# Opening stage of a two-layer trunk: modulation rows as four column-group products among the first part's, and the first part done one stream at a time

## The chip, the cores and the metric

The kernel runs on one core of one Trainium2 chip. The metric is the device time of one execution in microseconds (us), median of three runs. The engines are TensorE (PE in the rows, with its weight loads as PEld), VectorE (DVE), ScalarE (ACT), GpSimd (POOL) and SyncE (SP, which here only issues transfers).

## What is computed

Two layers run over 256 latent tokens ("x") and, in the first layer, 256 context tokens ("ctx"), each of width 1024. Every sub-layer is normalised and modulated by a shift and a scale that are products of a conditioning vector with `w_mod`. The opening stage computes the first modulation rows and the first tiles of the first feed-forward product:

```
silu_c = jax.nn.silu(c)
silu_cc = jax.nn.silu(c_ctx)
...
m = (silu_c @ w_mod[i] + b_mod[i]).reshape(b, 1, N_MOD, d)
mc = (silu_cc @ w_mod[i] + b_mod[i]).reshape(1, 1, N_MOD, d)
...
def modulate(x, g, shift, scale):
    return rms_norm(x, g) * (1 + scale) + shift

def swiglu(h, w13, w2):
    a, b = jnp.split(h @ w13, 2, axis=-1)
    return (jax.nn.silu(a) * b) @ w2
```

The rest (attention with pooling, a gated mixer, three more feed-forward blocks) is the same in both kernels.

## The kernel before

Activations lie transposed: 8 parts (k = 0 to 7) of 128 features, each with 512 columns, of which the first 256 are the latent stream and the last 256 the context stream. Large products are done in three matmuls: every fp32 operand is split into a rounded high part and a rest (`whi`/`wlo` or `sh`/`sl` for weights, `AH`/`AL` for activations; ACT rounds, DVE subtracts), and `mm3` adds wlo·AH, whi·AH and whi·AL in PSUM.

`start()` holds four weight tile pairs ("f" = 0 to 3, two tiles each, eight PSUM banks `pss`) and walks over the eight parts in the hand-written `order`. For part i of that order it needs its weights (512 KB, `raw4`, two buffers, split into hi and lo) and its normalised and modulated activations: DVE multiplies by `rb` (the reciprocal root mean square), ACT applies scale and shift into `h`, ACT rounds to `AH`, DVE subtracts to `AL`. Then 24 matmuls follow.

Scale and shift reach `mod` in two ways. For parts 0 to 4 DVE multiplies rows of `w_mod` (512 KB transfers, `wm`) with the conditioning vector, `cc`, and sums along the row (`use_mod`, L80): two rows by two streams for each part. For parts 5, 6 and 7 (`by_rows`) PE multiplies the 2-column conditioning vector by w_modr, four transfers of 768 KB with two of the eight contraction steps each (`wn`, lying in buffers called raw, raw, whi, wlo), 16 fp32 products of 384 columns (L697) that give 2 rows; ACT copies the rows out (L701), PE turns them into columns (L704), DVE copies them to `mod` (L707).

Ahead of that PE spreads the conditioning vector to `cc` (L665) and adds up the squares for the normalisation (L680). Order on an engine comes from a scheduler; where the code says `keep_in_program_order` (`pin`) it does not move. SP issues transfers in one queue, in program order, each behind the buffer that it overwrites. After `start()` the first feed-forward block goes on with tile pair f = 4 from `load_w`.

Of the kernel before, what the change touches and what calls it, by code (L numbers as in the profile page):

```python
# [16 lines left out]
P = 128  # L17
# [8 lines left out]
NR = 3  # L26
# [9 lines left out]
def trunk(ctx: ExitStack, tc: tile.TileContext, I, out):  # L36
# [8 lines left out]
    def bank():  # L45
        return pp.tile([P, 512], F32, name="ps")
# [592 lines left out]
    def start():  # L639
        ng = 4  # L640
        order = (0, 5, 1, 6, 2, 7, 3, 4)
        with tc.tile_pool(name="start", bufs=1) as sp:
# [6 lines left out]
            cT = sp.tile([P, 2, NK], F32, name="cT")  # L649
            nc.sync.dma_start(out=cT, in_=I["cT"])  # L650
# [5 lines left out]
            S.activation(out=cT, in_=cT, func=AF.Silu)  # L656

            S.activation(out=rb[:, 0:1], in_=cT[:, 0, 0:1], func=AF.Sqrt, scale=0.0, bias=epsb)

            for st in range(2):  # L660
                for h in range(2):
                    ps = bank()
                    for k4 in range(4):
                        k = 4 * h + k4
                        PE.matmul(ps[:, k4 * P:k4 * P + P], cT[:, st, k:k + 1].broadcast_to([P, P]),  # L665
                                  ident, start=True, stop=True)
# [14 lines left out]
            S.activation(out=rb, in_=ps, func=AF.Sqrt, scale=1.0 / D, bias=epsb)  # L681
# [3 lines left out]
            V.reciprocal(rb, rb)  # L685
# [5 lines left out]
            def by_rows():  # L691

                row = sp.tile([2, 2 * NR * P], F32, name="row")
                ps = [bank() for _ in range(2)]
                for k in range(NK):
# [4 lines left out]
                for j in range(2):  # L700
                    S.copy(row[:, j * NR * P:(j + 1) * NR * P], ps[j][0:2, :NR * P])  # L701
                ps = bank()
                for i in range(2 * NR):
                    PE.matmul(ps[:, 2 * i:2 * i + 2], row[:, i * P:i * P + P], ident[0:2, 0:2],  # L704
                              start=True, stop=True)
                for st in range(2):
                    V.tensor_copy(mod[:, st, :16].rearrange("p (j k) -> p j k", j=2)[:, :, NK - NR:],  # L707
                                  ps[:, 0:4 * NR].rearrange("p (j k s) -> p s j k", j=2, k=NR)[:, st])
                finish_mod(0, 0, 2, slice(NK - NR, NK))

            by_rows()
            pss = [[bank(), bank()] for _ in range(ng)]
            nxt = 1
            for i, k in enumerate(order):
                raw = raws.get(k) or get_raw(k)
                split(sh[:, k], sl[:, k], raw[:, :2])
                split(wh[0][:, k], wl[0][:, k], raw[:, 2])
                split(wh[1][:, k], wl[1][:, k], raw[:, 3])
                xr = tmp.tile([P, 2 * T], F32, name="sa", bufs=2)
                h = tmp.tile([P, 2 * T], F32, name="h32", bufs=2)  # L720
                V.tensor_tensor(out=xr, in0=X[:, k], in1=rb, op=ALU.mult)
                for st in range(2):
                    ts = slice(st * T, st * T + T)
                    S.activation(out=h[:, ts], in_=xr[:, ts], func=AF.Identity,
                                 scale=gs[:, st, 0, k:k + 1], bias=mod[:, st, k:k + 1])
# [6 lines left out]
                split(AH[:, k, :2 * T], AL[:, k, :2 * T], h)  # L732

                def products(f, k, first, last):
                    for ab in range(2):
                        cs = slice(ab * P, ab * P + P)
                        w = (sh[:, k, f, cs], sl[:, k, f, cs]) if f < 2 else \
                            (wh[f - 2][:, k, cs], wl[f - 2][:, k, cs])
                        mm3(pss[f][ab], *w, AH[:, k, :2 * T], AL[:, k, :2 * T], first, last)

                for f in range(ng):
                    products(f, k, i == 0, i == NK - 1)
# [17 lines left out]
def _pack(x, c, ctx, c_ctx, w_mod, b_mod, norm_g, ffn_w13, ffn_w2, w_in_a, qk_norm_g, pool_w,  # L760
# [5 lines left out]
    r["cT"] = ac(np.stack([c[0], c_ctx]).reshape(2, NK, P).transpose(2, 0, 1))  # L766
# [72 lines left out]
```

## Time and profile before

| what | value |
|---|---|
| median of 3 runs | 1141.48 us (1141.21 to 1141.87) |
| profiled execution | 1142.17 us |
| its span on the core | 1140.4 us |
| PE busy in the span | 1132.2 us (99%) |
| DVE, ACT, POOL busy | 863.6, 522.0, 68.4 us |
| granted TensorE clock | 1.00 |

The profiled execution took 1.8 us more than its span (what lies ahead of the first and behind the last instruction) and 0.7 us more than the median. The stage that changes is the first 73 us of the span. A matmul's duration in a row holds its way through the array; how fast matmuls follow each other is read from their starts.

### The profile page before, as it was taken

The numbers are of one execution on the slowest core, as the hardware profiler recorded it, in microseconds if no ns is written. First come the engines' busy times: TensorE is split into PE (matmuls) and PEld (weight loads), VectorE is DVE, ScalarE is ACT, GpSimd is POOL, SyncE is SP. The second block draws the span as 40 slices with busy tenths as digits, with TensorE's granted clock in tenths as the row PEclk, the third lists the DMA queues.
The fourth block names the chain that finished last, engine by engine and source line by source line (L and its number), as shares of the span: only waits on it lengthen the run. The fifth ranks groups of instructions, "written<-read, shape, count | busy, mean of one in ns | idle before, by whom it ended". The sixth has DMA issues, their size and how long they took to land.

```text
span 1140.4 us, 19165 instructions
## 1 busy us (share of the span) xinstructions
PE 1132.2 (99%) x7696; PEld 1033.9 (91%) x7696; DVE 863.6 (76%) x1582; ACT 522.0 (46%) x816; POOL 68.4 (6%) x140
## 2 busy tenths in 40 slices
PE   8999999999999999999999999999999999999998
PEld 4888888888888897899999999999999899999998
DVE  5967787878789979777778887656667788756663
ACT  5552212223223357664335456435445866434442
POOL 0000111122222200000000000000000000000000
PEclk9999999999999999999999999999999999999999
DMA  8844656788888850556687566456447536546543
GB/s 323 310 148 156 197 186 234 279 282 325 294 297 306 305 196 11 222 172 223 212 305 264 187 219 218 161 167 219 174 143 257 185 114 219 176 154 237 178 143 114
DMA packets 52408, 242.72 MB, mean 213 GB/s; under 512 B 5600, under 2 KB 11488, under 8 KB 38880
## 3 DMA queue, kind: packets, MB, share of 16 engines
q1 hardware_dynamic: 33888, 174.39, 43.4%
q0 software_dynamic: 18432, 67.12, 17.4%
q8 instruction: 60, 0.98, 0.4%
q14 instruction: 28, 0.23, 0.1%
HBM read 240.44 MB, written 1.05 MB: 212 GB/s over the span
## 4 chain that ended last, share of the span: by engine, by line
PE 97%; DVE 1%; ACT 1%; DMA 1%; issue 0%; SPq 0%; DVEq 0%; ACTq 0%
PE ps L148 30%; PE ps L149 30%; PE ps L150 30%; PE ps L697 1%; PE ps L618 1%; PE ps L619 1%; PE ps L617 1%; PE ps L680 1%; PE ps L665 1%; DMA raw<-in_w_out_a 0%; ACT whi L153 0%; PE ps L501 0%; PE ps L469 0%; DVE st L473 0%; PE ps L172 0%; ACT pe L477 0%
## 5 line engine op out<-in xcount | busy, mean ns | idle before, releaser
L148 PE MATMUL ps<-AH,wlo 128*128 128x258 f32 (+2 forms) x1664 | 507.1, 305 | 0.3 <-ACT AH L153 0.3
L149 PE MATMUL ps<-AH,whi 128*128 128x258 f32 (+2 forms) x1664 | 506.6, 305 | 0.0
L150 PE MATMUL ps<-AL,whi 128*128 128x258 f32 (+2 forms) x1664 | 505.5, 305 | 0.0
L153 ACT CAST whi<-raw 128x1024 fp32r<-128x1024 f32 (+2 forms) x354 | 313.7, 921 | 363.7 <-PE ps L150 260.3
L154 DVE TENSOR_TENSOR wlo<-raw,whi 128x1024 fp32r<-128x1024 f32 (+2 forms) x354 | 367.6, 1064 | 54.4 <-ACT whi L153 53.4
L148 PEld LDWEIGHTS ps<-AH,wlo 128*128 128x128 f32 x1664 | 316.3, 190 | 16.1 <-issue 1.1
L149 PEld LDWEIGHTS ps<-AH,whi 128*128 128x128 f32 x1664 | 314.3, 189 | 14.7 <-issue 0.5
L150 PEld LDWEIGHTS ps<-AL,whi 128*128 128x128 f32 x1664 | 313.4, 189 | 14.5 <-issue 0.2
L150 PE MATMUL ps<-HL,whi 128*128 128x256 f32 (+1 forms) x704 | 218.0, 310 | 0.0
L149 PE MATMUL ps<-HH,whi 128*128 128x256 f32 (+1 forms) x704 | 218.0, 310 | 0.0
L148 PE MATMUL ps<-HH,wlo 128*128 128x256 f32 (+1 forms) x704 | 218.0, 310 | 0.0
L80 DVE CUSTOM_DVE_ANT_0 wm<-wm,cc 128x1024 f32<-128x1024 f32 x138 | 164.7, 1219 | 6.1 <-DMA wm<-in_w_mod 5.0
L148 PEld LDWEIGHTS ps<-HH,wlo 128*128 128x128 f32 x704 | 132.5, 188 | 7.8
L150 PEld LDWEIGHTS ps<-HL,whi 128*128 128x128 f32 x704 | 132.5, 188 | 7.7
L149 PEld LDWEIGHTS ps<-HH,whi 128*128 128x128 f32 x704 | 132.6, 188 | 7.7
L72 POOL DMA_DIRECT2D wm<-in_w_mod x128 | 67.7, 529 | 546.2 <-DVE mod L80 508.6
L206 ACT ACTIVATE sa<-sa,cb 128x256 f32<-128x256 f32 x66 | 33.6, 510 | 119.7 <-DVE sa L205 116.4
L246 DVE SCALAR_TENSOR_TENSOR X<-ps,gate,X 128x256 f32<-128x256 f32 x64 | 30.9, 482 | 48.0 <-PE ps L150 47.9
L204 DVE COPY cb<-ps 128x1 f32<-128x1 f32 x66 | 10.3, 155 | 72.8 <-PE ps L150 72.7
L212 DVE TENSOR_TENSOR h<-ps,sa 128x512 f32<-128x512 f32 x22 | 15.2, 692 | 43.4 <-PE ps L150 34.2
L80 DVE CUSTOM_DVE_ANT_0 junk<-wm,cc 128x1024 bf16<-128x1024 f32 x34 | 41.4, 1218 | 8.6 <-ACT cc L667 7.2
L154 DVE TENSOR_TENSOR HL<-h,HH 128x256 fp32r<-128x256 f32 (+1 forms) x88 | 42.3, 485 | 0.0
(162 smaller groups left out, 705.3 us busy)
## 6 DMA issues: line engine op xcount, KB each, us to landing
raw<-in_w SPq DMA_DIRECT2D x84, 1024.0 KB, 4.9
wm<-in_w_mod POOLq DMA_DIRECT2D x128, 512.0 KB, 5.0
raw<-in_w SPq DMA_DIRECT2D x64, 704.0 KB, 4.1
wm<-in_w_mod SPq DMA_DIRECT2D x10, 512.0 KB, 6.4
raw<-in_w_in_a SPq DMA_DIRECT2D x5, 1024.0 KB, 7.8
raw<-in_w SPq DMA_DIRECT2D x8, 512.0 KB, 5.3
raw<-in_w_out_a SPq DMA_DIRECT2D x4, 1024.0 KB, 5.0
raw<-in_w_in_cu SPq DMA_DIRECT2D x4, 1024.0 KB, 4.8
```

What stands on the lines that cost most here:

```text
L72: eng.dma_start(out=w, in_=I["w_mod"][layer, i])
L80: pin(V.tensor_tensor_reduce(out=res, in0=w, in1=cc[:, st, :], scale=1.0, scalar=0.0, op0=ALU.mult, op1=ALU.add, accum_out=mod[:, 2 * laye ...
L148: PE.matmul(ps, wl, xh, start=first, stop=False)
L149: PE.matmul(ps, wh, xh, start=False, stop=False)
L150: PE.matmul(ps, wh, xl, start=False, stop=last)
L153: S.copy(hi, src)
L154: pin(V.tensor_tensor(out=lo, in0=src, in1=hi.bitcast(F32), op=ALU.subtract))
L206: S.activation(out=sa[:, :T], in_=sa[:, :T], func=AF.Silu, bias=cb[:, 0:1])
L212: V.tensor_tensor(out=h32[:, :n], in0=ps[1][:, :n], in1=sa[:, :n], op=ALU.mult)
L246: V.scalar_tensor_tensor(out=X[:, m, :T], in0=ps[:, :T], scalar=gate[:, 2 * layer, sub, m:m + 1], in1=X[:, m, :T], op0=ALU.mult, op1=ALU.add)
L617: PE.matmul(ps[b], AL[:, k, ts], hi[:, ws], start=(k == 0), stop=False)
L618: PE.matmul(ps[b], AH[:, k, ts], hi[:, ws], start=False, stop=False)
```

## The change

- The conditioning vector is kept as 32 columns for each contraction step (`c32`, two real ones and 30 zeros), so that a product fills 32 rows of its output. Step k goes to the rows 32·g to 32·g+31 of a bank, with g = k mod 4: four products stand side by side in a bank, in four groups of array columns. The `row` tile has 128 rows, and a small selector matrix (`sel`, loaded together with the conditioning vector as `cs`) adds the four groups up when the rows are turned (L715 of the changed kernel).
- Of the code's order, the products of the rows (L707) stand behind the first part's roundings and ahead of its matmuls; the first part (i = 0) is done a stream (256 columns) at a time, first three tile pairs, for one stream and then the other, then the fourth pair. All that leads to it is cut in halves as well: root, reciprocal, normalisation, and `AH` comes straight from ACT.
- The `raw4` of part 0 and that of the second part are issued ahead of w_modr and of the next `wm`. The order of parts is 0, 5, 6, 1, 7, 2, 3, 4 instead of 0, 5, 1, 6, 2, 7, 3, 4, and the 24 matmuls of a middle part go hi·AH, lo·AH, hi·AL over all tiles. The `use_mod` work stands behind the matmuls of its part.

```
-        order = (0, 5, 1, 6, 2, 7, 3, 4)
+        order = (0, 5, 6, 1, 7, 2, 3, 4)
...
+            c32 = sp.tile([P, NK, 32], F32, name="c32")
+            V.memset(c32, 0.0)
...
-            S.activation(out=cT, in_=cT, func=AF.Silu)
+            S.activation(out=c32[:, :, 0:2], in_=cs[:, :2 * NK].rearrange("p (k s) -> p k s", k=NK),
+                         func=AF.Silu)
...
+            raws = {0: get_raw(0)}
             for i in range(4):
                 nc.sync.dma_start(out=wn[i], in_=I["w_modr"][:, 2 * i:2 * i + 2])
-            raws = {0: get_raw(0)}
+            raws[order[1]] = get_raw(order[1])
             wm.update({(1, h): load_mod(0, 2 + h, nc.sync) for h in range(2)})
-            raws[order[1]] = get_raw(order[1])
...
-            S.activation(out=rb, in_=ps, func=AF.Sqrt, scale=1.0 / D, bias=epsb)
+            halves = [slice(st * T, st * T + T) for st in range(2)]
+            for ts in halves:
+                S.activation(out=rb[:, ts], in_=ps[:, ts], func=AF.Sqrt, scale=1.0 / D, bias=epsb)
...
+            def rows():
+                for r in range(2):
                     for j in range(2):
-                        PE.matmul(ps[j][0:2, :NR * P], cT[:, :, k],
-                                  wn[k // 2][:, k % 2, j * NR * P:(j + 1) * NR * P],
-                                  start=k == 0, stop=k == NK - 1)
...
+                        for g in range(4):
+                            k = 4 * r + g
+                            PE.matmul(psr[j][32 * g:32 * g + 32, :NR * P], c32[:, k],
+                                      wn[k // 2][:, k % 2, j * NR * P:(j + 1) * NR * P],
+                                      start=r == 0, stop=r == 1)
...
-                    PE.matmul(ps[:, 2 * i:2 * i + 2], row[:, i * P:i * P + P], ident[0:2, 0:2],
+                    PE.matmul(ps[:, 2 * i:2 * i + 2], row[:, i * P:i * P + P], sel,
...
+            for ts in halves:
+                pin(V.reciprocal(rb[:, ts], rb[:, ts]))
+                pin(V.tensor_tensor(out=xr0[:, ts], in0=X[:, order[0], ts], in1=rb[:, ts],
+                                    op=ALU.mult))
...
+                if i == 0:
+
+                    for ts in halves:
+                        normed(ts, AH[:, k, ts])
+                        normed(ts, h[:, ts])
+                        if ts.start == 0:
+                            for j in range(2):
+                                pin(S.copy(row[:, j * NR * P:(j + 1) * NR * P], psr[j][:, :NR * P]))
+                    for ts in halves:
+                        pin(V.tensor_tensor(out=AL[:, k, ts], in0=h[:, ts],
+                                            in1=AH[:, k, ts].bitcast(F32), op=ALU.subtract))
...
+                if i == 0:
+                    for fs, ts in ((range(ng - 1), 0), (range(ng - 1), 1), ((ng - 1,), 0), ((ng - 1,), 1)):
...
+                if 0 < i < NK - 1:
+                    for a, x in ((0, AH), (1, AH), (0, AL)):
+                        for f in range(ng):
+                            for ab in range(2):
+                                PE.matmul(pss[f][ab], tile_of(f, ab, k)[a], x[:, k, :2 * T],
+                                          start=False, stop=False)
```

Three places show what the scheduler makes of it. The rows name the operation, out<-in and the output's size, and in brackets the engines and transfers that it waits for (DMAHW0 is the transfer of the conditioning vector).

ACT at the very start, before:

```order
L656 ACT_TABLE_LOAD
L656 ACTIVATE cT<-cT 128x16 [waits DMAHW0_49]
L658 ACT_TABLE_LOAD [waits DVE_49]
L658 ACTIVATE rb<-cT,epsb 128x1 [waits Activation_49]
L667 COPY cc<-ps 128x512 [waits PE_49]
```

The same of the changed kernel (c_87 is `c32`):

```order
L660 ACT_TABLE_LOAD [waits DMAHW0_49]
L660 ACTIVATE c_87<-cs 128x8x2 [waits DVE_49]
L663 ACT_TABLE_LOAD
L663 ACTIVATE rb<-c_87,epsb 128x1 [waits Activation_49]
L672 COPY cc<-ps 128x512 [waits PE_49]
```

The first activation now has two things to wait for, and the wait for the transfer moved ahead of the table load.

PE from the third w_modr transfer on, before (`raw`, `whi`, `wlo` of L697 are the four buffers of w_modr):

```order
L697 MATMUL ps<-whi,cT 2x384 [waits DMAHW3_49]
L697 MATMUL ps<-whi,cT 2x384 x3
L697 MATMUL ps<-wlo,cT 2x384 [waits DMAHW4_49]
L697 MATMUL ps<-wlo,cT 2x384 x3
L704 MATMUL ps<-ident,row 128x2 [waits Activation_49]
L704 MATMUL ps<-ident,row 128x2 x2
L148 MATMUL ps<-AH,sl 128x512 [waits DVE_49,PE_49]
L149 MATMUL ps<-AH,sh 128x512
L150 MATMUL ps<-AL,sh 128x512
```

The same stretch of the changed kernel, behind six L787 matmuls of AH with sh and whi:

```order
L787 MATMUL ps<-AL,sh 128x256 [waits DVE_49]
L787 MATMUL ps<-AL,sh 128x256
L707 MATMUL ps<-whi,c_87 32x384 [waits DMAHW4_49]
L707 MATMUL ps<-whi,c_87 32x384 x3
L787 MATMUL ps<-AL,sh 128x256 x2
L787 MATMUL ps<-AL,whi 128x256 x2
L787 MATMUL ps<-AH,sl 128x256 [waits DVE_49]
L787 MATMUL ps<-AH,sl 128x256 x3
L787 MATMUL ps<-AH,wlo 128x256 [waits DVE_49]
L707 MATMUL ps<-wlo,c_87 32x384 [waits DMAHW5_49]
L707 MATMUL ps<-wlo,c_87 32x384 x3
L787 MATMUL ps<-AH,wlo 128x256
```

Half of the row products now stand behind matmuls that need the first stream's AL from DVE.

DVE from the first part's AL on, before:

```order
L154 TENSOR_TENSOR AL<-h_227,AH 128x512 [waits Activation_49]
L154 TENSOR_TENSOR sl<-raw_131,sh 128x512 [waits DMAHW5_49,Activation_49]
L154 TENSOR_TENSOR wlo<-raw_131,whi 128x256 [waits Activation_49] x2
L80 ISA junk,mod<-wm,cc 128x1024 [waits DMAHW6_49]
L80 ISA mod 128x1
L80 ISA wm,mod<-wm,cc 128x1024 [waits DVE_49]
L80 ISA mod 128x1
L707 COPY mod<-ps 128x2x3 [waits PE_49]
L707 COPY mod<-ps 128x2x3
```

The same of the changed kernel:

```order
L758 TENSOR_TENSOR AL<-h_209,AH 128x256 [waits Activation_49]
L762 TENSOR_TENSOR sl<-raw_129,sh 128x512 [waits DMAHW1_49]
L762 TENSOR_TENSOR wlo<-raw_129,whi 128x256 x2
L765 TENSOR_TENSOR sa<-X,rb 128x512 [waits DMAHW5_49]
L758 TENSOR_TENSOR AL<-h_209,AH 128x256 [waits Activation_49]
L718 COPY mod<-ps 128x2x3 [waits PE_49]
L718 COPY mod<-ps 128x2x3
L154 TENSOR_TENSOR sl<-raw_135,sh 128x512 [waits DMAHW6_49,Activation_49]
L92 TENSOR_TENSOR mod<-mod,par 128x2x2x3 [waits DVE_49]
L154 TENSOR_TENSOR wlo<-raw_135,whi 128x256 [waits Activation_49]
L98 SCALAR_TENSOR_TENSOR gs<-mod,par 128x2x3 [waits DVE_49]
L80 ISA junk,mod<-wm,cc 128x1024 [waits DMAHW7_49]
```

The L80 pair that stood ahead of the row copies now stands behind them, and behind the second stream's AL. Behind the last row shown, up to the normalisation (`sa`) of the third part, come three more L80, one AL and one sl of 512 columns, three wlo of 256 and one L92 and L98 each. The order outside this stage is the same in both kernels.

## Rows read from the trace of the kernel before

**Rows 1.** The page: span, busy times, PE and granted clock in 40 slices.
```profile
span 1140.4 us, 19165 instructions
PE 1132.2 (99%) x7696; PEld 1033.9 (91%) x7696; DVE 863.6 (76%) x1582; ACT 522.0 (46%) x816; POOL 68.4 (6%) x140
...
PEclk9999999999999999999999999999999999999999
```

**Rows 2.** Windows of the opening: stretch, length, PE, PEld, DVE, ACT, POOL busy, clock, DMA.
```profile
9.46:16.65 7.19, 7.19 (x17) 2.20 (x15) 4.07 (x10) 4.37 (x7) 0.00 (x0) 1.00 1.03 420
16.65:27.06 10.41, 10.41 (x33) 2.64 (x32) 8.95 (x11) 4.00 (x8) 0.00 (x0) 1.00 0.86 321
27.06:34.42 7.36, 7.36 (x37) 6.01 (x37) 5.53 (x17) 4.88 (x12) 0.00 (x0) 1.00 0.75 267
34.42:39.97 5.55, 5.55 (x25) 4.50 (x24) 5.55 (x11) 2.97 (x8) 0.00 (x0) 1.00 0.89 292
39.97:73.30 33.33, 33.33 (x146) 27.05 (x144) 28.13 (x56) 19.08 (x36) 2.24 (x4) 1.00 0.69 236
```

**Rows 3.** Timeline of DVE: start, duration, instruction, count, idle time before and its end.
```profile
17.48 3.35 DVE L685 RECIPROCAL rb<-rb 128x512 f32<-128x512 f32 x1 [1.85 <-ACT rb L681]
...
29.57 0.23 DVE L707 COPY mod<-ps 128x6 f32<-128x6 f32 x2 [1.83 <-PE ps L704]
...
57.02 1.22 DVE L80 CUSTOM_DVE_ANT_0 wm<-wm,cc 128x1024 f32<-128x1024 f32 x1
...
58.16 0.42 DVE L154 TENSOR_TENSOR wlo<-raw,whi 128x256 fp32r<-128x256 f32 x1
58.50 0.16 DVE L92 TENSOR_TENSOR mod<-mod,par 128x4 f32<-128x4 f32 x1
58.57 0.42 DVE L154 TENSOR_TENSOR wlo<-raw,whi 128x256 fp32r<-128x256 f32 x1
...
58.98 0.69 DVE L721 TENSOR_TENSOR sa<-X,rb 128x512 f32<-128x512 f32 x1
59.58 0.68 DVE L154 TENSOR_TENSOR sl<-raw,sh 128x512 fp32r<-128x512 f32 x1
...
64.36 0.68 DVE L154 TENSOR_TENSOR AL<-h,AH 128x512 fp32r<-128x512 f32 x1
```

**Rows 4.** Timeline of ACT, the start, the rows' copy and one part's activations.
```profile
0.73 1.28 ACT L656 ACT_TABLE_LOAD   x1 [0.73 <-PEq L830]
2.67 0.22 ACT L656 ACTIVATE cT<-cT 128x16 f32<-128x16 f32 x1 [0.65 <-DMA cT<-in_cT]
...
27.17 0.47 ACT L701 COPY row<-ps 2x384 f32<-2x384 f32 x1 [0.18 <-PE ps L697]
...
33.87 1.09 ACT L724 ACTIVATE h<-sa,mod,gs 128x256 f32<-128x256 f32 x2
34.99 0.62 ACT L153 CAST AH<-h 128x512 fp32r<-128x512 f32 x1
...
37.48 0.71 ACT L153 CAST whi<-raw 128x256 fp32r<-128x256 f32 x2
```

**Rows 5.** Timeline of PE: the start, the first turning products, matmuls of 258 columns.
```profile
3.31 6.15 PE L665 MATMUL ps<-ident,cT 128*128 128x128 f32 x32 [3.31 <-DMA ident<-in_ident]
...
27.06 0.82 PE L704 MATMUL ps<-ident,row 2*128 2x2 f32 x6
27.82 0.50 PE L148 MATMUL ps<-AH,sl 128*128 128x512 f32 x1
...
700.08 0.28 PE L149 MATMUL ps<-AH,whi 128*128 128x258 f32 x1
700.19 0.28 PE L150 MATMUL ps<-AL,whi 128*128 128x258 f32 x1
```

**Rows 6.** Timeline of PE in attention: fp32 products in two column groups (128*64).
```profile
465.61 0.65 PE L501 MATMUL ps<-pt,VV 128*64 128x256 f32 x2 [0.51 <-ACT pt L493]
...
466.31 1.51 PE L501 MATMUL ps<-pt,VV 128*64 128x256 f32 x12
...
467.72 0.76 PE L377 MATMUL ps<-ident,ri 128*64 128x128 f32 x5
468.41 0.39 PE L148 MATMUL ps<-AH,wlo 128*128 128x256 f32 x1
```

**Rows 7.** The last w_modr transfer: issue on SP, and us to landing.
```profile
8.92 0.33 SPq L672 DMA_DIRECT2D wlo<-in_w_modr  x1
...
wlo<-in_w_modr SPq DMA_DIRECT2D x1, 768.0 KB, 11.6
```

More of the change, by code (lines that the diff above doesn't have):

```diff
@@ L655, in start @@
             wm[0, 1] = load_mod(0, 1, nc.sync)
-            S.activation(out=cT, in_=cT, func=AF.Silu)
-            S.activation(out=rb[:, 0:1], in_=cT[:, 0, 0:1], func=AF.Sqrt, scale=0.0, bias=epsb)
+            S.activation(out=c32[:, :, 0:2], in_=cs[:, :2 * NK].rearrange("p (k s) -> p k s", k=NK),
+                         func=AF.Silu)
+            S.activation(out=rb[:, 0:1], in_=c32[:, 0, 0:1], func=AF.Sqrt, scale=0.0, bias=epsb)
             for st in range(2):
@@ L664, in start @@
                         k = 4 * h + k4
[L665 removed]
+                        PE.matmul(ps[:, k4 * P:k4 * P + P], c32[:, k, st:st + 1].broadcast_to([P, P]),
                                   ident, start=True, stop=True)
@@ L709, in by_rows @@
                 finish_mod(0, 0, 2, slice(NK - NR, NK))
-            by_rows()
-            pss = [[bank(), bank()] for _ in range(ng)]
+            pin = tc.keep_in_program_order
+            xr0 = tmp.tile([P, 2 * T], F32, name="sa", bufs=2)
+            for ts in halves:
+                pin(V.reciprocal(rb[:, ts], rb[:, ts]))
+                pin(V.tensor_tensor(out=xr0[:, ts], in0=X[:, order[0], ts], in1=rb[:, ts],
+                                    op=ALU.mult))
+            k = order[0]
@@ L713, in start @@
+            first = ((sh[:, k], sl[:, k], raws[k][:, :2]),) + tuple(
+                (wh[i][:, k], wl[i][:, k], raws[k][:, 2 + i]) for i in range(2))
+            for w, _, r in first:
+                pin(S.copy(w, r))
+            rows()
+            pss = []
             nxt = 1
@@ L715, in start @@
                 raw = raws.get(k) or get_raw(k)
[L716 to L719, printed above, removed]
-                h = tmp.tile([P, 2 * T], F32, name="h32", bufs=2)
[L721 to L725, printed above, removed]
+                if i:
+                    split(sh[:, k], sl[:, k], raw[:, :2])
+                    split(wh[0][:, k], wl[0][:, k], raw[:, 2])
+                    split(wh[1][:, k], wl[1][:, k], raw[:, 3])
@@ new lines, in start, with normed @@
+                xr = tmp.tile([P, 2 * T], F32, name="sa", bufs=2) if i else xr0
+                h = tmp.tile([P, 2 * T], F32, name="h32", bufs=2)
+                def normed(ts, out):
+                    st = ts.start // T
+                    pin(S.activation(out=out, in_=xr[:, ts], func=AF.Identity,
+                                     scale=gs[:, st, 0, k:k + 1], bias=mod[:, st, k:k + 1]))
+                if i == 0:
[8 more added lines that the diff above has]
+                                            in1=AH[:, k, ts].bitcast(F32), op=ALU.subtract))
+                        if ts.start == 0:
+                            for w, l, r in first:
+                                pin(V.tensor_tensor(out=l, in0=r, in1=w.bitcast(F32),
+                                                    op=ALU.subtract))
+                else:
+                    V.tensor_tensor(out=xr, in0=X[:, k], in1=rb, op=ALU.mult)
+                    for ts in halves:
+                        normed(ts, h[:, ts])
@@ L731, in start @@
                     nxt += 1
[L732 to L742, printed above, removed]
+                if 0 < i < NK - 1:
+                    for a, x in ((0, AH), (1, AH), (0, AL)):
+                        for f in range(ng):
+                            for ab in range(2):
+                                PE.matmul(pss[f][ab], tile_of(f, ab, k)[a], x[:, k, :2 * T],
+                                          start=False, stop=False)
+                elif i:
+                    for f in range(ng):
+                        for ab in range(2):
+                            mm3(pss[f][ab], *tile_of(f, ab, k), AH[:, k, :2 * T], AL[:, k, :2 * T],
+                                False, True)
         return pss
```

40 lines of the change are left out of this document (27 added, 13 removed).

## The prediction

> **What bounds the kernel now.** I read the page first: PE is busy 1132.2 of 1140.4 us at a granted clock of 9 or more tenths in every slice [rows 1]. Then the opening's windows: PE is busy for the whole of each, the row products take 10.41 us (16.65 to 27.06), the first part with the turning of the rows 7.36, the second 5.55, the other six 33.33, and the first matmul of tile pair 4 starts at 73.30 [rows 2]. So a microsecond taken off PE here is a microsecond gained only if the engines that feed PE follow. That is the third view, DVE's timeline: after a wait of 1.83 us at 29.57 it runs on to its last AL at 64.36 [rows 3]; 5.55 of 5.55 us busy beside the second part [rows 2]. The last part's matmuls begin 5.55 us before 73.30, at 67.75, and that AL is done at 65.04 [rows 3]: DVE is 2.7 us ahead of PE, and a PE that comes earlier by more than that meets DVE. All that lies behind 73.30 keeps its order, so I count to that point.
>
> **The parts and their costs.**
>
> *Start of ACT.* Before, the 1.28 us table load runs while the conditioning vector is under way, and the activation follows the landing at 2.67 [rows 4]. Now the load waits for the landing: 2.67 + 1.28 + 0.22 = 4.17. PE's first product, at 3.31 behind `ident` [rows 5], comes at 4.2: +0.9 for everything on PE up to the end of the sums (16.65 [rows 2]), which moves to 17.55. No row of before shows this wait's cost; it is 0 at least (a load that doesn't block) and 1.28 at most; I take 0.9, from the order. The zeroing of `c32` lies in DVE's first 8 us without work and costs nothing.
>
> *Row products.* 16 products in 10.41 us is 0.65 each, as two passes of 0.325 for 384 columns [rows 2]. What column groups give is read in attention, where two groups alternate: 12 passes of 256 columns span 1.51 us, the last of them taking about 0.39 as the neighbours do, so starts are (1.51 - 0.39) / 11 = 0.10 apart [rows 6]; at 0.325 for 384 columns one group alone would need 0.22. Two run at once. A landed w_modr transfer holds two contraction steps, hence two groups, twice (two banks): 2 x 0.65 = 1.3 for its four products instead of 2.6, 5.2 for all. Changing between full products and groups costs too: from the last L377 (467.72 + 0.76 - 0.27 = 468.21, with 0.27 the duration of one) to the next full product is 0.20 against 0.12 between two L377 [rows 6], about 0.1 each way. I take 1.5 for each group of four that stands among other matmuls. The bounds are 0.65 (four at once) and 2.6 (one after another).
>
> *First part.* 48 matmuls of 256 columns replace 24 of 512. At 258 columns starts are 0.12 apart [rows 5], so 5.8 against 24 x 0.23 = 5.55: +0.25. The six turning products cost what they did, 0.8 and 0.8 [rows 5].
>
> *When the first stream is ready.* Sums end at 17.55. Before, the reciprocal began 0.83 us behind the sums' end (17.48 against 16.65); half a root saves some 0.2 (a rounding of 512 against one of 256 columns [rows 3, 4] for scale): 18.15. Half a reciprocal is 1.68: 19.85. Multiplication 0.42, activation 0.6 (1.09 for two [rows 4]): PE can begin the first part at 20.9, 6.9 us before the 27.82 of now [rows 5].
>
> *But then it waits.* DVE first does the second stream's reciprocal and multiplication (20.2 + 1.68 + 0.34), then AL of the first: 22.65. PE has done its six matmuls of AH by 21.6 and stands for 1 us. Then: two of AL to 22.9, the third group of rows 24.4 (landed long before), nine matmuls 25.5, the fourth group 27.0. Its transfer landed at 8.92 + 11.6 = 20.5 [rows 7]; behind the 512 KB of part 0 it lands some 1.3 later, at 21.8, which is hidden.
>
> *What is queued behind that.* ACT's copies of the rows stand ahead of the second stream's activations: 27.1 + 0.47 [rows 4] = 27.6 for the last, 0.5 + 0.6 for AH and `h`: 28.7. DVE has done the first part's lo splits and the second part's multiplication by 24.0 and then stands until 28.7, because AL of the second stream is next in its queue. That is 4.7 us without work, against 1.83 before.
>
> *The third part.* From 28.7 DVE has, before the third part's normalisation: 4 long L80 at 1.14 (57.02 to 58.16), 3 subtractions of 512 columns at 0.60, 5 of 256 at 0.335, and 6 small ones at 0.07 [rows 3] = 4.56 + 1.80 + 1.68 + 0.42 = 8.45, so it begins at 37.15 and ends at 37.85. ACT: 1.09 + one rounding of 0.3 + 0.62 [rows 4] = 2.0. The third part can begin on PE at 39.9. PE itself is ready earlier: turning done at 28.5, the 27 matmuls left of the first part to 31.8, the second part to 37.35. It waits 2.5 us and begins at 39.9. Before it began at 39.97 [rows 2].
>
> *From there.* 6 parts by 5.55 = 33.3, to 73.2. DVE stays close: up to the sixth part's normalisation there are 8 L80, 9 of 512, 6 of 256 and 3 small ones behind the third part's, 16.8 us, so that AH of it comes at about 56.5, and PE gets there at 39.9 + 3 x 5.55 = 56.55. I add 0.3 for waits there and in the last part. Sum: 73.5 against 73.30, +0.2.
>
> *Transfers and the rest.* The `wm` of part 1 land 1.3 us later (issued behind one more of 512 KB); DVE uses them from 30 on. Later `raw4` wait for buffers that DVE frees no later than before. Reordering within middle parts and the new order of parts costs nothing by itself: the same 24 matmuls by 0.23.
>
> The profiled execution of 1142.17 would come to 1142.4; against the median, 0.7 lower, 1141.48 + 0.2 to 0.4: **1141.8 us**.
>
> **The rivals.** No change by over 0.2% (2.3 us) can be told from none here.
>
> 1. *The column groups don't run at once* (slower). At 2.6 instead of 1.5 for a group of four, the two groups on the path cost 2.2 more, and the first two, one after another to 22.75, delay the matmuls of AH past DVE's 22.65 and add some 0.7. All of it reaches DVE's wait at 28.7 and so the end: +2.9, 1144.7. It decides as soon as a group of four takes over 2.5. Against it: 0.10 between starts in [rows 6]; for it: those are groups of 64 columns, not 32.
>
> 2. *TensorE's clock falls* (slower). PE now stands for over 1 us before 20.9, for 1 us before 22.65 and for 2.5 us before 39.9, where before it had none. The granted clock is 1.00 in every window and in attention too, where PE stands for 0.51 us [rows 1, 6]; no row has pauses like these. At half clock a stretch of 10 us of matmuls costs 5 us, of which the wait at 39.9 covers half: +2.5, 1144.3. The Trainium skill's page "TensorE: Matmul & The Clock Gate", Part 1, says that the full clock is earned by activity and is given back when PE idles; by that rule this rival would hold, and the trace can't show it.
>
> 3. *DVE's standstill is shorter* (faster). If DVE could begin its list 2.5 us sooner, PE would not wait at the third part and 73.5 became 71.0: 1139.3. It takes a fourth row group that ends by 24.5. Its transfer is there at 21.8, but PE's queue has it behind DVE's AL of 22.65, four matmul groups and the third row group. Four products at once save 0.65 twice: 1140.5. The same page, Part 3, has a 3-tile column pack run 2.38 times as fast as one after another; by it the rows would be quicker than my pairs only if all four steps were there, and rows of this case show two.
>
> 4. *The change does only the local thing and the early ACT wait doesn't occur*: -0.9 to 1140.9, still within 0.2%.
>
> **How the numbers follow.** Forecast with its rounding and the fourth case: 0.72 (its own range 1140.6 to 1143.0, from the ends of the ACT wait and the tail). Rival 1: 0.10, rival 2: 0.05, rival 3: 0.13, of which half stays within 2.3 us. Slower: rivals 1 and 2 and nothing else, 0.15. Faster 0.07. Same 0.78. The range from 1139.6 to 1144.7 takes in the unit price of four at once and of one after another, and leaves out about 1 in 10.
>
> **What would show it.** ACT: the table load at 2.7, the activation at 4. PE: first 256-column matmul at about 21, L707 four in about 1.5, a wait of 2 to 3 us ahead of the third part's first 512-column matmul at about 40, tile pair 4 at 73.2 to 74. DVE: idle from 24 to 28.7 for ACT, then none. It would be wrong if DVE's standstill were much shorter, if L707 starts stand 0.32 apart, or if a granted clock below 1 shows in the first 45 us.

## The result, and the profile after

The changed kernel takes 1146.11 us (median of 6, 1144.85 to 1149.64), the kernel before beside it 1141.52 (median of 6): ratio 1.0044, 95% interval 1.0034 to 1.0054. It is slower by 4.6 us; forecast were 1141.8 and, at 0.78, no change that can be told from none. Two of the six executions, those of 1149.32 and 1149.64, have a mean granted clock of TensorE of 0.996 and 0.997; the other four have 1.000 to three digits, as has the profiled one of the kernel before [rows 1]. The profiled one is of these: 1144.98, of which the span is 1143.2, 2.8 more than the span in [rows 1].

The page, as in [rows 1]:
```profile
span 1143.2 us, 19216 instructions
...
PE 1128.6 (99%) x7720; PEld 1033.2 (90%) x7720; DVE 864.0 (76%) x1586; ACT 521.7 (46%) x818; POOL 68.7 (6%) x140
...
PEclk9999999999999999999999999999999999999999
```
PE works 3.6 us less than before and the span is 2.8 longer: PE now waits. Where, the windows tell (columns as in [rows 2]; the stretches are rows and pause, first part, second part, third to seventh part, last part up to tile pair 4):
```profile
17.03:20.54 3.51, 2.65 (x17) 0.75 (x17) 2.87 (x3) 2.61 (x7) 0.00 (x0) 1.00 1.00 407
20.54:32.02 11.48, 10.62 (x76) 8.01 (x77) 7.14 (x18) 5.28 (x12) 0.00 (x0) 1.00 0.75 269
32.02:39.72 7.70, 5.83 (x26) 4.42 (x24) 7.70 (x17) 3.66 (x9) 0.00 (x0) 1.00 0.67 200
39.72:69.81 30.09, 28.42 (x121) 22.31 (x121) 26.55 (x54) 15.20 (x31) 2.25 (x4) 1.00 0.71 245
69.81:76.10 6.29, 5.92 (x25) 4.53 (x25) 4.11 (x7) 4.59 (x7) 0.00 (x0) 1.00 0.47 171
```
Up to 39.72 PE stands for 0.87, 0.86 and 1.87 us and yet the third part begins 0.25 earlier than the 39.97 of [rows 2]. Tile pair 4 begins at 76.10 instead of 73.30. So the whole 2.8 us of this execution are lost between 39.72 and 76.10, where DVE, busy without a gap from 28.5 to 58.3, suddenly stands idle.

PE's timeline at the start of the first part, then DVE's and PE's two known waits (answering to [rows 3, 5]):
```profile
17.03 2.65 PE L707 MATMUL ps<-raw,c 128*32 128x384 f32 x16
20.54 0.73 PE L787 MATMUL ps<-AH,sh 128*128 128x256 f32 x4 [0.87 <-ACT AH L746]
21.11 0.39 PE L787 MATMUL ps<-AH,whi 128*128 128x256 f32 x2
22.36 0.50 PE L787 MATMUL ps<-AL,sh 128*128 128x256 f32 x2 [0.86 <-DVE AL L758]
22.79 1.48 PE L707 MATMUL ps<-whi,c 128*32 128x384 f32 x8
```
```profile
28.49 0.42 DVE L758 TENSOR_TENSOR AL<-h,AH 128x256 fp32r<-128x256 f32 x1 [4.31 <-ACT h L746]
```
Then the place of the loss: SP's issues, the us from issue to landing of the last one, and what ACT, DVE and PE do after it.
```profile
47.49 0.38 SPq L645 DMA_DIRECT2D raw<-in_w  x1
47.96 0.46 SPq L129 DMA_DIRECT2D raw<-in_w  x1
53.95 0.38 SPq L645 DMA_DIRECT2D raw<-in_w  x1
...
raw<-in_w SPq DMA_DIRECT2D x1, 512.0 KB, 7.2
```
```profile
61.17 0.62 ACT L153 CAST sh<-raw 128x512 fp32r<-128x512 f32 x1 [3.51 <-DMA raw<-in_w]
```
```profile
58.20 0.08 DVE L80 DVE_READ_ACCUMULATOR2_ANT mod<- 128x1 f32 x1
61.83 0.69 DVE L154 TENSOR_TENSOR sl<-raw,sh 128x512 fp32r<-128x512 f32 x1 [3.54 <-ACT sh L153]
62.44 1.22 DVE L80 CUSTOM_DVE_ANT_0 wm<-wm,cc 128x1024 f32<-128x1024 f32 x1
...
67.29 0.69 DVE L765 TENSOR_TENSOR sa<-X,rb 128x512 f32<-128x512 f32 x1
```
```profile
69.81 0.50 PE L148 MATMUL ps<-AH,sl 128*128 128x512 f32 x1 [1.59 <-ACT AH L153]
...
70.90 0.50 PE L150 MATMUL ps<-AL,sh 128*128 128x512 f32 x1 [0.37 <-DVE AL L154]
```
The kernel before, at the same place: the last part's raw4 on SP, its us to landing, and its rounding on ACT.
```profile
52.48 0.38 SPq L645 DMA_DIRECT2D raw<-in_w  x1
...
raw<-in_w SPq DMA_DIRECT2D x1, 512.0 KB, 5.4
...
57.94 0.62 ACT L153 CAST sh<-raw 128x512 fp32r<-128x512 f32 x1 [5.86 <-DMA raw<-in_w]
```
The last part's raw4 is the L645 issued at 53.95 in the changed kernel. It waits for one of two buffers, which DVE frees with the sixth part's lo splits. Before, it is issued at 52.48; it now lands 7.2 us after its issue instead of 5.4. ACT rounds it at 61.17 instead of 57.94: 3.23 late. DVE asks for it at 58.28, 1.30 earlier than the 59.58 of [rows 3], because in its new list this split stands behind one long L80 of the sixth part and ahead of three. Before, the split had 1.0 us to spare (rounding done at 58.56). 3.23 + 1.30 - 1.0 is the 3.5 us that DVE stands, and three L80, an AL and the last part's normalisation wait behind the split. PE gets that part's AH at 69.81.

I took this transfer for the cause (theory 1). Rivals: ACT's later start (theory 2), DVE's standstill of 4.31 us at 24, which leaves no reserve (theory 3), and TensorE's clock, which the two longest executions point to (theory 4).

### The profile page after: what moved, and what is told of

Read it like the earlier page. It is cut to its first block, busy times and chain, and to the rows that moved or that the text cites. A ratio compares the mean times of both kernels' runs of the same rounds, so it can differ in the third digit from the quotient of the medians.

```text
span 1143.2 us, 19216 instructions
## 1 busy us (share of the span) xinstructions
PE 1128.6 (99%) x7720; PEld 1033.2 (90%) x7720; DVE 864.0 (76%) x1586; ACT 521.7 (46%) x818; POOL 68.7 (6%) x140
## 4 chain that ended last, share of the span: by engine, by line
PE 92%; DVE 4%; ACT 1%; DMA 1%; issue 0%; ACTq 0%; DVEq 0%
PE ps L150 29%; PE ps L148 29%; PE ps L149 29%; DVE wm L80 1%; DVE junk L80 1%; PE ps L618 1%; PE ps L619 1%; PE ps L617 1%; PE ps L685 1%; DMA raw<-in_w 1%; DVE wlo L154 1%; PE ps L670 1%; DMA raw<-in_w_out_a 0%; ACT whi L153 0%; PE ps L501 0%
## 5 line engine op out<-in xcount | busy, mean ns | idle before, releaser
L148 PE MATMUL ps<-AH,wlo 128*128 128x258 f32 (+2 forms) x1636 | 496.0, 304 | 0.3 <-ACT AH L153 0.3
L149 PE MATMUL ps<-AH,whi 128*128 128x258 f32 (+2 forms) x1636 | 495.6, 303 | 0.0
L150 PE MATMUL ps<-AL,whi 128*128 128x258 f32 (+2 forms) x1636 | 494.5, 304 | 0.0
L148 PEld LDWEIGHTS ps<-AH,wlo 128*128 128x128 f32 x1636 | 311.0, 190 | 14.9 <-issue 1.1
L149 PEld LDWEIGHTS ps<-AH,whi 128*128 128x128 f32 x1636 | 309.0, 189 | 13.5 <-issue 0.5
L150 PEld LDWEIGHTS ps<-AL,whi 128*128 128x128 f32 x1636 | 308.2, 189 | 13.2 <-issue 0.2
L80 DVE CUSTOM_DVE_ANT_0 wm<-wm,cc 128x1024 f32<-128x1024 f32 x138 | 164.8, 1220 | 5.8 <-DMA wm<-in_w_mod 5.0
L80 DVE CUSTOM_DVE_ANT_0 junk<-wm,cc 128x1024 bf16<-128x1024 f32 x34 | 41.4, 1219 | 8.5 <-ACT cc L672 7.6
```

The lines of the kernel that those rows point to most:

```text
L80: pin(V.tensor_tensor_reduce(out=res, in0=w, in1=cc[:, st, :], scale=1.0, scalar=0.0, op0=ALU.mult, op1=ALU.add, accum_out=mod[:, 2 * laye ...
L148: PE.matmul(ps, wl, xh, start=first, stop=False)
L149: PE.matmul(ps, wh, xh, start=False, stop=False)
L150: PE.matmul(ps, wh, xl, start=False, stop=last)
```

## The experiments

Time by granted clock of the executions; "full" is a mean that shows as 1.000, "lower" 0.996 to 0.999. Ratios are to the kernel before beside it.

| kernel | median us | ratio [95%] | full: number, median | lower: number, median |
|---|---|---|---|---|
| changed, first time | 1146.11 | 1.0044 [1.0034, 1.0054] | 4, 1145.07 | 2, 1149.48 |
| l_after (changed again) | 1146.99 | 1.0033 [1.0021, 1.0045] | 3, 1146.45 | 3, 1147.43 |
| a_raw3 | 1144.86 | 1.0026 [1.0016, 1.0035] | 4, 1143.64 | 6, 1146.13 |
| e_pool | 1145.21 | 1.0023 [1.0012, 1.0033] | 4, 1142.05 | 6, 1145.90 |
| b_table | 1146.59 | 1.0044 [1.0031, 1.0056] | 0 | 5, 1146.59 |
| d_copies | 1145.69 | 1.0035 [1.0022, 1.0047] | 0 | 5, 1145.69 |
| f_fill | 1146.24 | 1.0032 [1.0019, 1.0044] | 3, 1144.67 | 2, 1147.22 |
| g_poolfill | 1142.23 | 0.9999 [0.9991, 1.0008] | 10, 1142.27 | 1, 1141.68 |
| q_third | 1142.49 | 1.0012 [1.0003, 1.0020] | 8, 1142.21 | 4, 1144.72 |
| r_first | 1143.20 | 1.0009 [1.0000, 1.0017] | 11, 1143.20 | 0 |
| h_rows | 1143.46 | 1.0012 [1.0003, 1.0021] | 0 | 11, 1143.46 |
| h_fill | 1142.01 | 0.9994 [0.9985, 1.0003] | 1, 1140.76 | 10, 1142.11 |
| n_best | 1141.06 | 0.9993 [0.9984, 1.0002] | 7, 1140.95 | 4, 1143.69 |
| p_best | 1141.43 | 0.9996 [0.9988, 1.0005] | 11, 1141.43 | 0 |
| k_best | 1148.16 | 1.0052 [1.0039, 1.0064] | 0 | 5, 1148.16 |
| k2 | 1149.09 | 1.0047 [1.0034, 1.0060] | 1, 1145.51 | 4, 1149.17 |

The kernel before beside them: 91 executions, all full.

**The last transfer: a_raw3 and e_pool.**
```
-                raw = sp.tile([P, ng, 2 * P], F32, name="raw4", bufs=2)
+                raw = sp.tile([P, ng, 2 * P], F32, name="raw4", bufs=3)
```


> One edit to the changed kernel: a third raw4 buffer, so that the last part's transfer no longer waits until DVE has done the sixth part's lo splits; DVE's and PE's order stay as they are. Theory 1 (the 2.8 us come from that late transfer, for which DVE's split of the last part stands 3.5 us with three long L80 behind it): issue before 50 us instead of 53.95, landing before 58, no DVE wait for it at 61.8, tile pair 4 at 73.0 to 73.6 instead of 76.10, time 2.5 to 3 us under the changed kernel's, 1142.0 to 1142.6, which can't be told from the kernel before. Rival (DVE is simply full after its 4.3 us standstill at 24, so any order of transfers ends alike): tile pair 4 stays at 75.5 or later, 1144.5 to 1146.


```
-            use_mod(layer, i, load_mod(layer, i, nc.gpsimd), tc.keep_in_program_order)
+            use_mod(layer, i, load_mod(layer, i, nc.sync if (layer, i) < (0, 18) else nc.gpsimd), tc.keep_in_program_order)
```


> One edit to the changed kernel: the first two modulation columns that POOL requests (at 51.27 and 53.89 us, while the last raw4 is under way) are requested on SP's queue instead, the second of them behind the last raw4. It also moves DVE's split of that part two long L80 later in its queue. If the transfer is slow because POOL's packets share the DMA engines with it: it lands in 5 us or less instead of 7.2, and with the split further back DVE waits under 0.5 us; tile pair 4 at 73 to 74, 1142 to 1143. If it is slow because of the 1 MB weight transfer ahead of it in its own queue: still 6 to 7 us; the wait is then about 1 to 1.5 us, since the split stands 2.3 us later, and the time about 1143.5 to 1144.5.

SP's, DVE's and PE's timelines of a_raw3, then DVE's and PE's of e_pool with its last raw4 transfer:
```profile
48.27 1.38 SPq L645 DMA_DIRECT2D raw<-in_w  x2
...
59.98 0.69 DVE L154 TENSOR_TENSOR sl<-raw,sh 128x512 fp32r<-128x512 f32 x1
...
71.02 0.39 PE L148 MATMUL ps<-AH,sl 128*128 128x512 f32 x1
```
```profile
61.28 1.22 DVE L80 CUSTOM_DVE_ANT_0 wm<-wm,cc 128x1024 f32<-128x1024 f32 x1
62.42 0.68 DVE L154 TENSOR_TENSOR sl<-raw,sh 128x512 fp32r<-128x512 f32 x1
...
67.27 0.39 PE L148 MATMUL ps<-AH,sl 128*128 128x512 f32 x1
...
raw<-in_w SPq DMA_DIRECT2D x1, 512.0 KB, 6.3
```
In both the wait for the transfer is gone, by two different ways, and so is PE's wait ahead of the last part. At full clock that is worth 1.4 us (a_raw3) and 3.0 us (e_pool), and e_pool is then level with the kernel before (1142.05; before 1141.89). This bears out theory 1 and speaks against theory 3 as the cause of the 2.8: DVE's standstill is still there. In e_pool the transfer took 6.3 us instead of 7.2; most of that kernel's gain is the split's place in DVE's list, now behind three more long L80. The Trainium skill, "Trainium Kernel Development and Optimization", Key Constraints, has transfers from SP's and POOL's queues run interleaved on the same 16 engines; the profile after agrees: between 53 and 55 us 109 packets of POOL's queue and 38 of SP's took 64.4% and 22.0% of the engines' time.

How much of the 7.2 is due to POOL is not shown. Of my two expectations for e_pool, 6.3 fits the one that blames the 1 MB of weights ahead in SP's own queue. By the profiles these weights land 0.3 us after the raw4's issue in the kernel before (44.47 and 8.3 us, against 52.48), 0.8 in e_pool (47.53 and 6.8, against 53.52) and 2.1 in the changed kernel (47.96 and 8.1, against 53.95), and the raw4 takes 5.4, 6.3 and 7.2. POOL's transfers were under way beside it before, too (issued at 51.35 and 55.65).

Both medians missed what I expected; 6 of 10 executions of each ran at a lower clock. a_raw3 missed at full clock as well: 1143.64, where 1142.0 to 1142.6 was expected. These executions lie 1.75 above the kernel before. The only profile of a_raw3 is one at the lower clock, so what costs that stays open.

**The clock: the changed kernel again, and PE's pauses filled.**

> The changed kernel once more, unedited, for its spread. If PE's pauses take its clock down in some executions only: about half of them at a mean granted clock of 0.996 to 0.999, and these 2 to 4.5 us slower than the others, which stay at 1144.8 to 1147. If the two slow executions seen before were chance: all at 1.000 and 1144.8 to 1147.

Three of six were at the lower clock this time. Its profile is one of them; PE's timeline, and windows (columns as before, the last but two is the granted clock):
```profile
4.57 6.51 PE L670 MATMUL ps<-ident,c 128*128 128x128 f32 x32 [4.57 <-DMA ident<-in_ident]
...
18.27 1.51 PE L707 MATMUL ps<-raw,c 128*32 128x384 f32 x16
21.79 0.73 PE L787 MATMUL ps<-AH,sh 128*128 128x256 f32 x4 [2.00 <-ACT AH L746]
...
23.61 0.58 PE L787 MATMUL ps<-AL,sh 128*128 128x256 f32 x2 [0.85 <-DVE AL L758]
24.12 2.77 PE L707 MATMUL ps<-whi,c 128*32 128x384 f32 x8
```
```profile
22.00:24.00 2.00, 1.15 (x8) 0.85 (x7) 1.97 (x4) 0.23 (x1) 0.00 (x0) 0.97 1.03 399
24.00:26.00 2.00, 2.00 (x7) 0.56 (x8) 1.43 (x4) 0.00 (x0) 0.00 (x0) 0.50 0.31 120
26.00:28.00 2.00, 2.00 (x12) 1.18 (x9) 0.00 (x0) 0.00 (x0) 0.00 (x0) 0.67 0.94 283
28.00:30.00 2.00, 2.00 (x15) 0.83 (x13) 0.00 (x0) 0.66 (x2) 0.00 (x0) 1.00 0.93 304
```
`ident` landed later, PE reached the rows 1.24 later, and by then both transfers were there: the eight products took 1.51 us instead of 2.65. So the pause behind them is 2.00 us instead of 0.87, and after it and the next one of 0.85 the clock is at 0.50, that is 1.2 GHz instead of 2.4. The next four products take 2.77 instead of 1.48. The last part begins 3.0 later than in the profile above: 1.25 from the late start, the rest behind the fall. The executions at full clock took 1144.63 to 1146.72, about as expected; the lower ones are by their medians only 1.0 longer here, where 2 to 4.5 was expected, and 4.4 the first time.

The filling, in three places of the first parts (core of it; `z` is 128x128 zeros). The kernels with it also hold the first eight row products in the code's order, q_third and r_first below among them:
```
+            def fill(n, out, x, start=False):
+                for i in range(n):
+                    pin(PE.matmul(out, z.rearrange("p k c -> p (k c)"), x, start=start and i == 0,
+                                  stop=False))
...
+                        fill(7, pss[0][0][:, :T], wh[1][:, order[0]], True)
...
+                                fill(7, pss[0][0][:, ts], AH[:, k, ts])
...
+                    fill(8, pss[0][0], AH[:, order[0], :2 * T])
```


> The changed kernel with PE's three pauses filled: 7 matmuls of 256 columns with zero weights between the first two row groups and the third (0.84 us by 0.12 each), 7 more ahead of the first AL, 8 of 512 columns (1.84 us by 0.23) ahead of the third part; they add nothing to the sums, and DVE, ACT and SP keep their order. If the granted clock falls because PE pauses there: no execution below a mean granted clock of 0.9995, all of them within 1 us of each other at 1144.5 to 1145.5, the late last transfer being still there (a pause of about 1.6 us ahead of the last part at 69.8 stays). If the falls come of something else (the chip, the transfers): some executions at 0.996 to 0.998 and 1147 to 1150 as before.

> The same filling in the kernel with POOL's first two requests on SP's queue. Without it that kernel took 1141.7 to 1142.2 in its executions at full clock and 1144.3 to 1146.7 in the others. Two causes, transfer and clock, and nothing else: all executions at 1141.5 to 1142.5, no clock below 0.9995, the same as the kernel before. If the slow executions have a third cause, 1144 or more shows again.

g_poolfill came out as expected by its median: 1142.23, the kernel before's time. One of its 11 executions shows 0.999, and they spread more than expected, 1141.08 to 1143.34; without filling the same kernel went to 1146.73. f_fill missed: two of five at 0.999 and 1146.66 and 1147.77. Its pause of 1.60 us ahead of the last part at 69.14 was left, and its profile has a wait far behind the opening that none of the theories had: 1.65 us at 896 for an AL; ahead of it ACT had waited 3.58 us for a weight transfer. So with the transfer late, filling the opening alone doesn't help; with the transfer mended, it does. (e_pool and g_poolfill ran on two different chips, the next two side by side on a third; the kernel before was all at full clock on each.)

Which pause does it, told apart in e_pool with the third filling alone and with the first two alone:

> The kernel with POOL's first two requests on SP's queue (which varied from 1141.7 to 1146.7), with only PE's wait ahead of the third part filled (8 zero-weight matmuls of 512 columns, 1.84 us); the two pauses at 20 to 22 us stay. If the early pauses are what takes the clock down: executions at 0.997 to 0.999 and 1143.5 to 1146 remain, half or more of them. If it is the 1.86 us ahead of the third part: all at 1.000, 1141.1 to 1143.

> The same kernel with only the two pauses at 20 to 22 us filled (7 and 7 matmuls of 256 columns), the 1.86 us ahead of the third part left. If the early pauses are what takes the clock down: all at 1.000 and 1141.1 to 1143. If the third: as many executions below 0.9995 as without filling, 1143.5 or more. If both: some in each of the two kernels.

With only the third filled, 4 of 12 executions are lower, fewer than the half that was expected; with only the early two filled, none of 11. r_first's time missed, though: 1143.20, with six of 11 above the 1143 that was expected, about 1 above g_poolfill and the full-clock executions of q_third. It still has the third pause, at full clock:
```profile
39.21 1.19 PE L813 MATMUL ps<-AH,sh 128*128 128x512 f32 x4 [1.68 <-ACT AH L153]
```
So, as far as 12 and 11 executions tell, the early pauses start the falls. But a wait ahead of the third part can be followed by one too: in the profile of a_raw3, where an early fall came first, 1.86 us at 41.50 were, with a granted clock of 0.65 in 42 to 45, and in that of b_table 1.85 at 42.97.

**ACT's start and DVE's standstill: b_table and d_copies.**
```
+            S.activation(out=rb[:, 1:2], in_=epsb, func=AF.Silu)
```


> One edit to the changed kernel: a Silu of one column of constants stands first on ACT, so that the table is loaded before the conditioning vector lands. PE's first product comes at about 3.3 instead of 4.04. Everything up to the third part hangs on that start, so all of it moves 0.7 earlier, the last raw4 transfer too. If only the size of that start was wrong (the theory that the early ACT wait is what costs): 0.7 us or more off, but the DVE wait for the last transfer stays at about 3.5 us, and the time stays 2 us or more above before, 1144. If the late transfer is a matter of a few tenths (it meets POOL's transfer by chance): the wait shrinks by more than 0.7 and the time falls to 1142 or 1143.


```
                     for ts in halves:
                         normed(ts, AH[:, k, ts])
                         normed(ts, h[:, ts])
-                        if ts.start == 0:
-                            for j in range(2):
-                                pin(S.copy(row[:, j * NR * P:(j + 1) * NR * P], psr[j][:, :NR * P]))
+                    for j in range(2):
+                        pin(S.copy(row[:, j * NR * P:(j + 1) * NR * P], psr[j][:, :NR * P]))
```


> One edit to the changed kernel: ACT's two copies of the rows stand behind both streams' activations of the first part instead of between them, so DVE's AL of the second stream no longer waits for PE's last row products. DVE's idle time at 24 falls from 4.3 us to under 1, its list begins about 4 us sooner, PE gets the third part's AH when it is itself ready (37.4 to 38 instead of 39.72). The last raw4 is requested by as much sooner as DVE frees its buffer, 50 to 52. By the theory of the standstill as the root: tile pair 4 at 71 to 72, 1140 to 1141, under the kernel before. By the theory that only the last transfer counts and it is slowed by the other queues whenever it is issued: a DVE wait of over 2 us for it remains, tile pair 4 at 74 or later.

Neither gained what it was to gain. In both profiles `ident` landed 3.7 us after its issue (2.0 in the profile after) and PE began at 5.0, so b_table says nothing on the table load. Both had a first pause of 2.0 us and a clock of 0.62 to 0.63 in 23 to 27. In d_copies DVE's standstill only moved: it did more first, and then stood 5.89 us for the turned rows:
```profile
32.55 0.23 DVE L718 COPY mod<-ps 128x6 f32<-128x6 f32 x2 [5.89 <-PE ps L715]
```
All their executions being lower, theories 2 and 3 aren't told apart by them.

**The rows alone: h_rows, h_fill, n_best, p_best.** The row products in four column groups, put into the kernel before with its order of parts, its whole first part and its order of transfers:
```
-                for k in range(NK):
-                    for j in range(2):
-                        PE.matmul(ps[j][0:2, :NR * P], cT[:, :, k],
+                for r in range(2):
+                    for j in range(2):
+                        for g in range(4):
+                            k = 4 * r + g
+                            PE.matmul(ps[j][32 * g:32 * g + 32, :NR * P], c32[:, k],
...
```


> One part of the change alone, in the kernel before: the row products as four column groups (zero-padded weights of 32 columns, turned with sel), with the old order of parts, whole first part, whole reciprocal and the w_modr transfers ahead of part 0's. PE has the rows done at about 21 (last transfer 20.5) instead of 27, and must then wait some 2 us for the first part's AH (reciprocal 17.5 to 20.8, multiplication, activation, rounding: 23). If a pause of PE there takes the clock down: granted clock of half in the windows from 21 to 27, executions at 0.997, 1142 to 1145. If only the order and the late transfer made the change slow: full clock, DVE freed of its 1.83 us wait at 29.57, tile pair 4 at 71.5 to 73, 1139.8 to 1141.3.

All 11 executions are at 0.996 or 0.997. The profile has a pause of 2.19 us and behind it a clock of one half for some 7 us; the second pause, of 1.43, falls within these.
```profile
23.64 2.27 PE L711 MATMUL ps<-cs,row 128*128 128x2 f32 x12 [2.19 <-ACT row L708]
27.35 0.77 PE L148 MATMUL ps<-AH,sl 128*128 128x512 f32 x1 [1.43 <-DVE sl L154]
...
24.00:26.00 2.00, 1.91 (x11) 1.83 (x10) 0.05 (x1) 1.10 (x3) 0.00 (x0) 0.54 0.28 88
26.00:28.00 2.00, 0.65 (x2) 0.59 (x3) 1.93 (x8) 1.34 (x3) 0.00 (x0) 0.50 0.00 0
28.00:30.00 2.00, 2.00 (x6) 1.58 (x5) 2.00 (x4) 1.50 (x4) 0.00 (x0) 0.50 0.46 130
30.00:32.00 2.00, 2.00 (x8) 1.59 (x7) 2.00 (x5) 0.00 (x0) 0.00 (x0) 0.75 1.01 364
```
So the time saved on rows comes back as idle PE and then as slow PE, without any of the new order. With filling (core of it):
```
+                    pin(PE.matmul(pss[0][0][:, :P], ident, ones, start=True, stop=True))
```


> The row products alone in the kernel before (as in the run named h_rows), with PE's two pauses filled by products nobody reads: 5 of 128 columns between the rows and their turning, 4 between the turning and the first part, all into a bank that the first part then starts afresh. If the half clock from 24 to 31 us is what eats the gain of the faster rows: full clock in all executions, turning done at 25.0 instead of 25.9, nine matmuls of the first part at 0.23 instead of 0.42, together 2.6 us: 1140 to 1141.3 against 1143.46 without filling. If the rows gain nothing even at full clock (DVE is the bound): 1142 to 1143.

> The same, with a Silu of one column of constants first on ACT, so that the table is there when the conditioning vector lands. PE's start moves from 4.05 to 3.4 where the transfer of ident allows it (it landed between 3.2 and 4.9 in the profiles so far). If PE's chain from the start to the rows is still what sets the opening: 0.3 to 0.7 us less than without, 1139.5 to 1141. If DVE or the transfers set it: the same as without.

> The kernel with the rows alone, the early table load and fillings (n_best), whose executions at full clock took 1140.1 to 1141.2 and the others 1142.2 to 1144.5; its profile still had pauses of 0.85 us ahead of the last row products and 1.34 ahead of their turning. Here 3 products of 128 columns stand in the first and 10 instead of 5 in the second. If these pauses are what is left: all executions at full clock, 1140 to 1141.3, faster than the kernel before by about 0.1%. If not: 4 of 11 again at 0.997 or 0.998.

In h_fill five products of 128 columns took 1.38 us, less than the pause, and 1.57 were left; 10 of 11 executions stayed lower, so h_fill doesn't decide between its two expectations. n_best (ACT's early load: PE began at 3.55) got 7 of 11 to full clock, p_best with more filling in the two pauses left 11 of 11:
```profile
18.80 1.49 PE L714 MATMUL ps<-whi,c 128*32 128x384 f32 x8
20.22 0.94 PE L702 MATMUL ps<-ones,ident 128*128 128x128 f32 x6
21.08 1.49 PE L714 MATMUL ps<-wlo,c 128*32 128x384 f32 x8
22.50 2.50 PE L702 MATMUL ps<-ones,ident 128*128 128x128 f32 x20
24.83 1.40 PE L724 MATMUL ps<-cs,row 128*128 128x2 f32 x12
```
So the falls that n_best still had go with these pauses, as far as 11 executions tell. p_best's 1141.43 lies 0.5 under the kernel before, with an interval that holds 1; 1140 to 1141.3 was expected. n_best's seven executions at full clock, 1140.13 to 1141.17, all lie under the lowest of the kernel before beside it (1141.59), but they are picked by their clock. A version that surely beats both was not found.

**Two attempts on DVE's list.** Row copies last, one modulation column of part 1 on DVE ahead of the turned rows, two pauses filled; k_best also with all raw4 requested ahead of the weights of tile pair 4:

> An attempt at a version without the causes found: row copies behind both streams' activations, one of part 1's modulation columns (two long L80) on DVE ahead of the turned rows' copies so that DVE works through its 4.3 us standstill, all raw4 transfers requested ahead of the weights of tile pair 4 and later, and the first two pauses of PE filled with zero-weight matmuls. Expected: third part by 38 without a wait, tile pair 4 at 70.5 to 72, full clock, 1139 to 1141, faster than before by 0.05 to 0.2%. If DVE's list has another wait (for the turning, at 28.5): 1141 to 1143.

> The attempt named k_best without its edit on the order of transfers, which had the weights of tile pair 4 land too late: row copies behind both streams' activations, one modulation column of part 1 ahead of the turned rows' copies on DVE, two pauses of PE filled. If that order of transfers was its whole loss: no wait of 3.8 us ahead of tile pair 4, which starts at 72 to 73.5, 1141 to 1142. If the last raw4 is late again behind 1 MB of weights: a DVE wait of 2 us or more for it and 1143.5 to 1146.

Both lost by new waits for late data: PE 3.78 us at 76.8 for tile pair 4's weights in k_best, 4.01 at 65.2 for an AH in k2, ACT having waited 8.7 for a raw4. Nine of their ten executions were at a lower clock as well.

## Why the prediction was wrong

**Right**, in the profiled execution (forecast; measured): PE's start (4.2; 4.04), two column groups at once (1.5 for four products; 1.48), the first part at 20.9 (20.54), its waits of about 1 (0.87, 0.86), DVE's standstill until 28.7 (28.49), the third part at 39.9 (39.72), the sixth at 56.55 (56.53). Some of it is luck: in l_after, b_table and d_copies PE began at 4.57 to 5.04, behind `ident` and not behind ACT, and its first pause was 2.0.

**Wrong in its size: the tail.** "I add 0.3 for waits there and in the last part", on the ground that "later `raw4` wait for buffers that DVE frees no later than before". I had DVE's list by its length, not by its order: DVE freed the buffer 1.47 us later, the transfer took 1.8 longer, and the split was asked for 1.3 earlier. From the third part's start to tile pair 4 the sum had 33.3 and these 0.3; measured were 36.38 (39.72 to 76.10), so the term is 3.1. Tile pair 4 came 2.8 later than before (76.10 less 73.30) where the sum had 0.2, and e_pool, which takes the wait out, is 3.0 faster at full clock. The whole miss of the profiled execution is this.

**Wrong in its chance: rival 2.** The mechanism and its price stood there ("TensorE's clock falls", +2.5), at 0.05. It occurred in 5 of 12 executions and cost 1.0 to 4.4. It adds about 1 us to the first median (1146.11 against 1145.07 at full clock). I set the pauses against attention's 0.51, saw no row like them, and took that as evidence for no fall. In l_after 2.00 and 0.85 us, with little work between them, were followed by 0.50, and of 22 executions with them filled and the transfer mended one shows less than 1.000 (0.999). The page that I cited, the Trainium skill's "TensorE: Matmul & The Clock Gate", Part 1, by which an idle PE gives its full clock back, agrees with that in kind; but its advice on how long a pause may be would have let each of these pass, and there the measurement decides.

**Rivals 1, 3, 4**: the groups ran at once, the standstill was not shorter, and the wait of ACT occurred (0.7 us).

What stays open: what costs a_raw3 1.75 us at full clock; why f_fill, g_poolfill and r_first show 0.8 to 1.7 us of waiting at 893 to 896, and how much of the scatter at full clock is that (1144.63 to 1147.06 in the changed kernel); and what ACT's early table load is worth alone, since b_table began late for another reason.

## What to carry to other kernels

Work taken off an engine that others feed turns into pauses, and on TensorE a pause may cost more than itself: price it by the granted clock of several executions, not of one profile. A list that is worked in order has to be read up to its last transfer: who frees that buffer, when, and what stands behind the instruction that waits for it. If a saving can't be used, harmless products in the gap keep the clock, but they gain nothing by themselves.

## What the runs showed that I had not expected

- Four column groups ran at once in the profiles in which both transfers were there when the rows began: eight products in 1.51 us (l_after, 18.27) against 2.65 (profile after), though two at once had been forecast. Being faster lengthened the pause.
- Pauses of 0.87 and 0.86 us were followed by no fall, 1.42 and 0.85 (a_raw3) and 2.00 and 0.85 (l_after) by one each, 2.03 alone (b_table) by one, 1.68 behind 19 us without a pause (r_first) by none. The length alone doesn't decide: ahead of the third part 1.85 and 1.86 us (b_table, a_raw3) were followed by a fall, 1.87 and 1.88 (after, l_after) by none. After a fall the clock is at 1.2 GHz for some 3 to 7 us in the records: 24 to 27 in l_after, 24 to 31 in h_rows.
- The 64 KB of `ident`, issued at the same 1.2 us each time, landed after 1.9 to 3.7 us in the profiles. In the changed kernel the late ones (l_after, b_table, d_copies: 3.3 to 3.7) go with the first pauses of 2.0. That the kernel before would hide a late one behind DVE's 2.7 us of lead is my reading and not shown: in its only profile it landed after 2.0.
